# Queueing an expert's transposes, scatter and gather behind the products of the piece ahead, and ending every side of a branch with a product

## The chip, the cores and the metric

The kernel runs on one core of one Trainium2 chip. The metric is the device time of one execution in microseconds (us), as the median of several runs. One execution was also taken by the hardware profiler. It gives for each engine what ran when, at which line of the kernel, and what ended each wait. TensorE stands in its rows as PE (products and transposes, which are both matrix instructions) and PEld (the weight loads that go before them); VectorE is DVE, ScalarE is ACT, GpSimd is POOL. SP is the engine that issues the transfers. A name with q at its end (PEq, SPq) is the engine's sequencer, which takes branches, waits and loads of registers.

## The reference, cut to what matters

The reference is a two-layer backbone over 256 context and 256 latent tokens. The change touches only the feed-forward part of the second layer, which is a mixture of eight experts over the 256 latent tokens:

```python
def moe_swiglu(h, w_router, w_gate, w_up, w_down):
    logits = (h @ w_router).astype(jnp.float32)
    top_val, top_idx = lax.top_k(logits, TOP_K)          # 2 of 8 experts for each token
    top_w = jax.nn.softmax(top_val, axis=-1)
    gates = ...                                          # (tokens, 8), zero where not chosen
    out = jnp.zeros_like(h)
    for e in range(N_EXPERTS):
        out = out + gates[..., e:e + 1] * swiglu(h, w_gate[e], w_up[e], w_down[e])
    return out
```

`swiglu` is `(silu(h @ w_gate) * (h @ w_up)) @ w_down`, with 1024 x 3584 weights for gate and up and 3584 x 1024 for down, all in float32. The kernel computes for each expert only the tokens that chose it.

## The kernel before, in words

**Experts and slots.** The tokens of an expert are gathered into up to 128 slots. `gather` (line 1414) does it with products of the tokens and a one-hot matrix `P`. Slots 0 to 63 are part A and are always computed. Slots 64 to 127 are part B. How many tokens an expert has (`n_e`) is known only at run time: with at most 64 there is no part B, with 65 to 96 part B is computed as four "quarters" of 32 slots, with more as two "halves" of 64.

**Pieces.** The weights of an expert come in 21 pieces of 2 MB, 168 pieces for the eight experts, in a ring of 8 buffers (`raw`, lines 1443 to 1454). SP issues the transfer of a piece when the products that read the buffer eight pieces earlier are over. The inner width of 3584 is cut into stretches of 1024, 1024, 1024 and 512 columns. Numbered within an expert, the pieces are: 0 to 3 gate, gate, up, up of the first stretch; 4 to 7 the same of the second; 8 and 9 down of the first; 10 to 13 gate and up of the third; 14 and 15 down of the second; 16 gate and 17 up of the fourth; 18 and 19 down of the third; 20 down of the fourth.

**Products of one piece.** `prods` (line 1480) and `d_step` (line 1528) first run all of part A, eight or sixteen matrix products, each of which is two records in the trace. Then `rest_of` (line 1461) branches on `n_e`: with more than 64 tokens it runs the quarters or the halves of part B, otherwise nothing. So a piece of an expert with at most 64 tokens shows 16 records (32 in pieces 16 and 17), and one with quarters 48 (96). In this execution experts 1, 4, 5 and 7 have no part B and experts 0, 2, 3 and 6 run quarters.

**What lies between pieces.** After the last up piece of a stretch VectorE multiplies (`at`, line 1509). Then `act_t` (line 1513) transposes the product in TensorE (tiles `actA`, `actB`, line 1520), and the copies at lines 1525 and 1526 make it the left side of the down products. Further steps on TensorE are `rows_of` (tile `PT`, line 1432), the gather of the next expert (tile `gat`, line 1421), the scatter of the expert before (tile `sc`, lines 1627 and 1632; it too branches on `n_e`, and its last side runs products), and the load of `n_e` into a register of PE's sequencer (line 1669).

**Order.** The code names for each piece what is to run ahead of it: `act_t` before pieces 5, 9, 15 and 19, the scatter before piece 2, `rows_of` before 11, the gather before 14, the load of `n_e` before 0. That order is no queue order. The scheduler of the language puts an instruction into its engine's queue as early as its own model finds it ready, so in the trace these steps stand ahead of where the code has them: `act_t` straight after the last up piece, the scatter around pieces 0 and 1. A branch with all its sides is placed as one block.

Of the kernel before, what the change touches and what calls it, by code (L numbers as in the profile page):

```python
# [141 lines left out]
def kernel(  # L142
# [6 lines left out]
    V, S, G, PE, SP = nc.vector, nc.scalar, nc.gpsimd, nc.tensor, nc.sync  # L149
# [26 lines left out]
    def pst(name="ps"):  # L176
        tag = name if name in banks else "A"
        return cur["ps"].tile([128, 512], F32, tag=tag, name=name, bufs=banks[tag])
# [52 lines left out]
    last = {}  # L231
# [1040 lines left out]
    for g in range(2):  # L1272
        p = pst("shb")
        for k in range(4):
            PE.matmul(p[:, k * 128:(k + 1) * 128], modT[1][:, 24 + 4 * g + k, 0:1].to_broadcast([128, 128]), ident,
                      start=True, stop=True)
        S.copy(shb[g], p)
    shl = mb.tile([128, 32], F32, name="shl")[:, 0:8]
    p = pst("shl")
# [131 lines left out]
    def ptile(name):  # L1411
        return ptr.tile([128, 512], F32, tag="tr", name=name)
# [30 lines left out]
    def load(src):  # L1443

        n = npiece[0]
        npiece[0] += 1
        pool, bufs = (mwa, RA) if n % NR < RA else (mw, RB)
        raw = pool.tile(list(src.shape), F32, tag="raw", name="raw", bufs=bufs)
        if n < NR:
            with tc.issue_after(last["w"].ins):  # L1450
                SP.dma_start(raw, src)
        else:
            SP.dma_start(raw, src)
        return raw

    def wsel(w, e):
        if isinstance(e, int):
            return w[0, e]
        return w[0, bass.ds(e, 1)].rearrange("o a b -> (o a) b")

    def rest_of(n_e, quarters, halves):

        if n_e is None:
            halves()
            return
        with tc.If(n_e[0] > 64):  # L1466
            with tc.If(n_e[0] > 96) as br:
                halves()
            with br.Else():
                quarters()  # L1470


    STRETCH = ((0, 1024), (1024, 1024), (2048, 1024), (3072, 512))
# [1 line left out]
    def expert_steps(e, xT, done, n_e=None):  # L1475

        y = []
        at, acts = {}, {}

        def prods(p, xA, xB, w, start, stop):  # L1480

            nk = len(xA)
            n = w(0).shape[-1]

            def part(dst, x, parts):
                m, c = 128 // parts, n // parts
                for k in range(nk):
                    for i in range(parts):
                        PE.matmul(dst[m * i:m * i + m, 0:c], x[k][:, 0:m], w(k)[:, c * i:c * i + c], start=(start and k == 0),  # L1489
                                  stop=(stop and k == nk - 1), tile_position=(0, m * i))  # L1490

            part(p[:, 0], xA, 2)
            rest_of(n_e, lambda: part(p[:, 1], xB, 4), lambda: part(p[:, 1], xB, 2))

        def gu_step(m, wi, k0, nk, ps):
            width = STRETCH[m][1] // 2

            def use(raw):
                if k0 == 0:
                    ps[wi] = gu_t[wi]  # L1500
                x = xT()
                prods(ps[wi], [x[:, k0 + k, 0:64] for k in range(nk)], [x[:, k0 + k, 64:128] for k in range(nk)],
                      lambda k: raw[:, k, :], k0 == 0, k0 + nk == KD)
                if k0 + nk == KD:
                    if wi == 0:
                        at[m] = mt.tile([128, 2, 512], F32, tag="at", name="at", bufs=2)
                        S.activation(at[m][:, :, 0:width], ps[0][:, :, 0:width], AF.Silu)  # L1507
                    else:
                        V.tensor_tensor(at[m][:, :, 0:width], at[m][:, :, 0:width], ps[1][:, :, 0:width], op=ALU.mult)  # L1509

            return use

        def act_t(m):

            nb = STRETCH[m][1] // 256
            ps = [ptile("actA"), ptile("actB")]

            def tr(b, n):
                for i in range(n):
                    PE.transpose(ps[b][:, i * 128:(i + 1) * 128], at[m][:, b, i * 128:(i + 1) * 128], ident)  # L1520

            tr(0, nb)
            tr(1, nb)
            acts[m] = mt.tile([128, 2, 512], F32, tag="act", name="act", bufs=2)
            S.copy(acts[m][:, 0, 0:128 * nb], ps[0][:, 0:128 * nb])  # L1525
            V.tensor_copy(acts[m][:, 1, 0:128 * nb], ps[1][:, 0:128 * nb])

        def d_step(m, f0):
            def use(raw):
                if m == 0 and f0 == 0:  # L1530
                    y.append(y_t)
                nf = STRETCH[m][1] // 128
                b = acts[m]
                end = m == 3

                def act(part, parts):

                    w = 128 // parts
                    per = nf // parts
                    return [b[:, part, f % per * 128 + f // per * w:f % per * 128 + f // per * w + w] for f in range(f0, f0 + 4)]  # L1540

                def part(i, parts):
                    w, c = 128 // parts, 1024 // parts
                    x = act(i, parts)
                    for k in range(4):
                        for j in range(parts):
                            PE.matmul(y[0][w * j:w * j + w, i, 0:c], x[k], raw[:, k, c * j:c * j + c],  # L1547
                                      start=(m == 0 and f0 == 0 and k == 0), stop=(end and k == 3), tile_position=(0, w * j))

                part(0, 2)  # L1550
                rest_of(n_e, lambda: part(1, 4), lambda: part(1, 2))
                if end:
                    ys = mt.tile([128, 2, 512], F32, tag="ys", name="ys", bufs=1)
                    S.copy(ys[:, 0], y[0][:, 0])
                    V.tensor_copy(ys[:, 1], y[0][:, 1])
                    done.append(ys)

            return use

        late_t = []  # L1560

        def pre():
            if late_t:
                m = late_t.pop(0)
                return lambda: act_t(m)
            return None

        for m in range(5):
            if m < 4:
                c0, width = STRETCH[m]  # L1570
                nk = 4 * 1024 // width
                ps = {}
                for wi in range(2):
                    w = wsel((moe_w_gate, moe_w_up)[wi], e)[:, c0:c0 + width]
                    for k0 in range(0, KD, nk):
                        src = w[k0 * 128:(k0 + nk) * 128].rearrange("(k p) f -> p k f", p=128)
                        yield src, (pre() if k0 else None), gu_step(m, wi, k0, nk, ps)
                late_t.append(m)
            if m > 0:
                c0, width = STRETCH[m - 1]  # L1580
                for f0 in range(0, width // 128, 4):
                    src = wsel(moe_w_down, e)[c0 + f0 * 128:c0 + (f0 + 4) * 128, :].rearrange("(k p) d -> p k d", p=128)
                    yield src, (pre() if f0 else None), d_step(m - 1, f0)

    def run_pieces(gen):
        for src, pre, use in gen:
            raw = load(src)
            if pre:
                pre()
            use(raw)  # L1590

    def residual():

        for g in range(2):
            for j in range(2):
                p = ptile("hrow")
                for k in range(4):
                    PE.transpose(p[:, k * 128:(k + 1) * 128], hT[:, 4 * g + k, 256 + 128 * j:384 + 128 * j], ident)
                S.copy(acc(j, g), by2(p))
        for g in range(2):  # L1600
            p = ptile("gfb")
            for k in range(4):
                PE.matmul(p[:, k * 128:(k + 1) * 128], modT[1][:, 40 + 4 * g + k, 0:1].to_broadcast([128, 128]), ident,
                          start=True, stop=True)
            S.copy(res(g), by2(p))
# [49 lines left out]
    def all_pieces():  # L1655
# [36 lines left out]
        run_last.append(pend)  # L1692

    run_pieces(all_pieces())
    run_last[0]()

    n_rv = nc.values_load(nmax_i[0:1, 0:1], min_val=0, max_val=256)
    with tc.If(n_rv > CAP):
# [4 lines left out]
        with tc.For_i(0, NE, 1) as ev:  # L1703
# [9 lines left out]
            rk, m = lambda j: col[:, j, 0:1], lambda j: col[:, j, 1:2]  # L1713
# [46 lines left out]
```

## Time and profile before

| | |
|---|---|
| median of 3 runs | 2031.52 us (2029.23, 2031.52, 2031.91) |
| profiled execution, its own time | 2026.94 us |
| span of its instructions | 2025.2 us |
| TensorE busy with products, of the span | 93% |
| mean granted TensorE clock | 0.978 of 2.4 GHz |
| from the first expert product to the end of the last | 1072.2 us to 2007.5 us |
| weights of the experts | 168 pieces of 2048 KB |

The profile's times are from the start of the span. A busy TensorE is not yet a TensorE at its peak, and the share is an average over the whole kernel; the experts, which the change touches, are the last 950 us.

### The profile page before, as it was taken

What the parts mean: (1) busy time and instruction counts of PE and PEld (TensorE: products, weight loads), DVE (VectorE), ACT (ScalarE), POOL (GpSimd) and SP (SyncE); (2) the same over time, 40 slices, a digit from 0 to 9 for tenths busy, and PEclk for the clock granted to TensorE, in tenths of its full rate; (3) what the DMA queues carried; (4) which work ended last, traced back from release to release, by engine and by line L of the source; (5) the groups of instructions that cost most, each with busy time, mean ns of one, the idle gap of its engine ahead of it and who ended that gap; (6) DMA issues with size and microseconds to landing.
All of it is one profiled execution on the core that took longest, in us unless ns stands there. A gap on an engine that the chain in (4) does not pass through costs nothing. (4 is left out here: it accounts for less than half of the span.)

```text
span 2025.2 us, 29234 instructions
## 1 busy us (share of the span) xinstructions
PE 1889.1 (93%) x12351; PEld 1124.2 (56%) x12351; DVE 685.3 (34%) x1333; ACT 431.0 (21%) x747; POOL 199.9 (10%) x245
## 2 busy tenths in 40 slices
PE   5999999999999999999989999899999888999996
PEld 3767754667888887877464443334344343434432
DVE  5874545353333335875541112110110212111112
ACT  3323433242222224334420100000000000000000
POOL 0542221010000000562300000000000000000000
PEclk9998998999999999999989999999999999999998
DMA  9333332535333333332576889999889999999993
GB/s 321 79 115 115 125 125 73 187 100 176 100 94 96 102 117 91 99 88 99 173 291 254 329 297 388 406 404 344 325 295 358 366 404 408 403 408 404 368 398 125
DMA packets 262343, 478.50 MB, mean 236 GB/s; under 512 B 16144, under 2 KB 142096, under 8 KB 262032
## 3 DMA queue, kind: packets, MB, share of 16 engines
q1 hardware_dynamic: 262160, 475.76, 65.0%
q8 instruction: 151, 2.47, 0.5%
q14 instruction: 32, 0.26, 0.0%
HBM read 474.68 MB, written 1.05 MB: 235 GB/s over the span
## 5 line engine op out<-in xcount | busy, mean ns | idle before, releaser
L1489 PE MATMUL u<-raw,xT 128*64 128x512 f32 (+3 forms) x2048 | 258.2, 451 | 7.6 <-issue 3.3
L1547 PE MATMUL y<-raw,act 128*64 128x512 f32 (+1 forms) x1792 | 260.0, 492 | 3.4 <-PEq L1466 2.5
L1489 PE MATMUL g<-raw,xT 128*64 128x512 f32 (+3 forms) x2048 | 256.6, 450 | 2.5 <-PEq L1466 2.3
L1509 DVE TENSOR_TENSOR at<-at,u 128x1024 f32<-128x1024 f32 (+1 forms) x32 | 34.8, 1088 | 518.2 <-PE u L1489 302.2
L256 ACT CAST wh<-raw 128x1024 fp32r<-128x1024 f32 (+1 forms) x129 | 133.0, 1039 | 324.9 <-PE mm L266 169.8
L257 DVE TENSOR_TENSOR wl<-raw,wh 128x1024 fp32r<-128x1024 f32 (+1 forms) x129 | 159.4, 1240 | 115.9 <-ACT wh L256 91.6
L1489 PEld LDWEIGHTS u<-raw,xT 128*64 128x64 f32 (+1 forms) x2048 | 105.4, 124 | 159.4 <-issue 141.4
L1489 PEld LDWEIGHTS g<-raw,xT 128*64 128x64 f32 (+1 forms) x2048 | 101.1, 123 | 148.4 <-issue 128.5
L1547 PEld LDWEIGHTS y<-raw,act 128*64 128x64 f32 (+1 forms) x1792 | 88.9, 123 | 156.0 <-issue 140.6
L1507 ACT ACTIVATE at<-g 128x1024 f32<-128x1024 f32 (+1 forms) x32 | 29.4, 917 | 340.7 <-PE g L1489 185.8
L266 PE MATMUL mm<-ah,wh 128*128 128x512 f32 (+1 forms) x400 | 101.3, 388 | 0.0
L266 PE MATMUL mm<-al,wh 128*128 128x512 f32 (+1 forms) x400 | 95.9, 376 | 0.0
L1728 POOL TENSOR_TENSOR rs<-ss,mhalf 128x1 f32<-128x1 f32 x2 | 1.1, 564 | 952.2 <-DVE ss L1727 952.2
L266 PE MATMUL mm<-ah,wl 128*128 128x512 f32 (+1 forms) x400 | 93.0, 372 | 0.0
L266 PEld LDWEIGHTS mm<-ah,wh 128*128 128x128 f32 x400 | 70.3, 191 | 20.2 <-issue 6.2
L266 PEld LDWEIGHTS mm<-al,wh 128*128 128x128 f32 x400 | 70.9, 189 | 13.9 <-issue 0.8
L1525 ACT COPY act<-actA 128x512 f32<-128x512 f32 (+1 forms) x32 | 17.0, 533 | 287.0 <-PE actA L1520 287.0
L266 PEld LDWEIGHTS mm<-ah,wl 128*128 128x128 f32 x400 | 70.5, 188 | 12.9
L1159 DVE SCALAR_TENSOR_TENSOR hT<-mm,mod,hT 128x256 f32<-128x256 f32 x72 | 31.8, 480 | 94.8 <-PE mm L266 69.1
L371 POOL TENSOR_TENSOR rs<-ms,mhalf 128x4 f32<-128x4 f32 (+1 forms) x8 | 8.8, 1103 | 473.9 <-DVE ms L369 473.9
L1520 PE MATMUL actA<-cs,at 128*128 128x128 f32 x112 | 19.2, 289 | 38.6 <-DVE at L1509 38.6
L266 PE MATMUL s<-ah,wh 128*128 128x512 f32 x192 | 47.6, 390 | 0.0
(424 smaller groups left out, 2556.4 us busy)
## 6 DMA issues: line engine op xcount, KB each, us to landing
raw<-in_moe_w_gate_dram SPq DMA_DIRECT2D x56, 2048.0 KB, 12.5
raw<-in_moe_w_up_dram SPq DMA_DIRECT2D x56, 2048.0 KB, 12.1
raw<-in_moe_w_down_dram SPq DMA_DIRECT2D x56, 2048.0 KB, 13.2
raw<-in_w_ada_dram SPq DMA_DIRECT2D x64, 512.0 KB, 4.8
raw<-in_w_in_dram SPq DMA_DIRECT2D x44, 512.0 KB, 3.8
raw<-in_ffn_w_gate_dram SPq DMA_DIRECT2D x22, 512.0 KB, 3.8
raw<-in_ffn_w_up_dram SPq DMA_DIRECT2D x22, 512.0 KB, 3.8
adaw<-in_w_ada_dram SPq DMA_DIRECT2D x10, 1024.0 KB, 7.8
```

The costliest lines, as they stand in the source:

```text
L256: S.copy(wh, raw)
L257: V.tensor_tensor(wl, raw, wh, op=ALU.subtract)
L266: PE.matmul(p, uk, a(k)[hl], start=(n == 0), stop=(n == len(seq) - 1))
L371: G.tensor_tensor(r[:, j0:j1], ms[:, j0:j1], mhalf[:, j0:j1], op=ALU.pow)
L1159: V.scalar_tensor_tensor(hT[:, m, c0:c1], p[:, c0:c1], modT[l][:, 8 * gi + m, i:i + 1], hT[:, m, c0:c1], op0=ALU.mult, op1=ALU.add)
L1489: PE.matmul(dst[m * i:m * i + m, 0:c], x[k][:, 0:m], w(k)[:, c * i:c * i + c], start=(start and k == 0), stop=(stop and k == nk - 1), tile ...
L1507: S.activation(at[m][:, :, 0:width], ps[0][:, :, 0:width], AF.Silu)
L1509: V.tensor_tensor(at[m][:, :, 0:width], at[m][:, :, 0:width], ps[1][:, :, 0:width], op=ALU.mult)
L1520: PE.transpose(ps[b][:, i * 128:(i + 1) * 128], at[m][:, b, i * 128:(i + 1) * 128], ident)
L1525: S.copy(acts[m][:, 0, 0:128 * nb], ps[0][:, 0:128 * nb])
L1547: PE.matmul(y[0][w * j:w * j + w, i, 0:c], x[k], raw[:, k, c * j:c * j + c], start=(m == 0 and f0 == 0 and k == 0), stop=(end and k == 3), ...
L1728: G.tensor_tensor(rs[:, j:j + 1], ss[:, j:j + 1], mhalf[:, 0:1], op=ALU.pow)
```

## The change

Two things change. `rest_of` gets the last product step of part A (the last of the 128-row blocks of the contraction, `k`) and issues it inside the branch, on every side of it, so that no side is empty. And `run_pieces` issues what is to run ahead of a piece behind the last product of part A that stands before the branch of the piece ahead: `tc.issue_after(ins)` adds an edge of order, without a wait, from `ins` to every TensorE instruction that the block makes. Instructions of other engines are not held by it. The scatter of the last expert stands outside and is as before.

```diff
-    def rest_of(n_e, quarters, halves):
+    def rest_of(n_e, last_a, quarters, halves):
+        def halves_(b=halves):
+            last_a()
+            b()
         if n_e is None:
-            halves()
+            halves_()
             return
-        with tc.If(n_e[0] > 64):
-            with tc.If(n_e[0] > 96) as br:
-                halves()
-            with br.Else():
-                quarters()
+        with tc.If(n_e[0] > 64) as b1:
+            with tc.If(n_e[0] > 96) as b2:
+                halves_()
+            with b2.Else():
+                halves_(quarters)
+        with b1.Else():
+            last_a()
...
-            def part(dst, x, parts):
+            def part(dst, x, parts, ks=range(nk)):
...
-            part(p[:, 0], xA, 2)
-            rest_of(n_e, lambda: part(p[:, 1], xB, 4), lambda: part(p[:, 1], xB, 2))
+            part(p[:, 0], xA, 2, range(nk - 1))
+            pe = last["pe"]
+            rest_of(n_e, lambda: part(p[:, 0], xA, 2, (nk - 1,)), lambda: part(p[:, 1], xB, 4), lambda: part(p[:, 1], xB, 2))
+            last["pe"] = pe
...
-                part(0, 2)
-                rest_of(n_e, lambda: part(1, 4), lambda: part(1, 2))
+                part(0, 2, range(3))
+                pe = last["pe"]
+                rest_of(n_e, lambda: part(0, 2, (3,)), lambda: part(1, 4), lambda: part(1, 2))
+                last["pe"] = pe
...
     def run_pieces(gen):
         for src, pre, use in gen:
             raw = load(src)
-            if pre:
+            if pre and last.get("pe"):
+                with tc.issue_after(last["pe"].ins):
+                    pre()
+            elif pre:
                 pre()
             use(raw)
+        last["pe"] = None
```

## Rows read from the trace of the kernel before

**Rows 1.** The page's first part: busy time, share of the span and instructions of TensorE's products.

```profile
PE 1889.1 (93%) x12351; PEld 1124.2 (56%) x12351; DVE 685.3 (34%) x1333; ACT 431.0 (21%) x747; POOL 199.9 (10%) x245
```

**Rows 2.** Windows of the experts' stage: the stretch, its length, busy time and instructions of each engine, granted clock, share of the time in which the DMA engines were busy, and GB/s.

```profile
1500.00:1600.00 100.00, 94.51 (x845) 42.74 (x838) 14.35 (x24) 5.43 (x9) 0.00 (x0) 1.00 0.88 328
...
1605.00:1700.00 95.00, 83.36 (x421) 34.15 (x418) 16.86 (x28) 7.01 (x11) 1.00 1.03 405
1700.00:1800.00 100.00, 92.55 (x547) 37.65 (x549) 16.34 (x28) 7.52 (x11) 1.00 1.03 406
1800.00:1900.00 100.00, 94.59 (x916) 42.27 (x908) 10.91 (x19) 5.95 (x9) 1.00 1.02 398
```

**Rows 3.** TensorE's waits from 1060 us to the end: who waited for whom, us in total, times, the longest.

```profile
PE actA L1520 <- DVE at L1509: 38.6, 29, 1.8
PE sc L1627 <- ACT ys L1554: 6.1, 8, 0.8
...
PE sc L1627 <- PEq L1466: 2.7, 4, 0.7
...
PE PT L1432 <- ACT act L1525: 2.0, 7, 0.3
```

**Rows 4.** TensorE in order of time in expert 2, which runs quarters: start, length, line, what is written and read, records, and the idle time before with what ended it.

```profile
1320.75 10.97 PE L1489 MATMUL u<-raw,xT 128*64 128x512 f32 x96
1333.13 0.66 PE L1520 MATMUL actA<-cs,at 128*128 128x128 f32 x4 [1.42 <-DVE at L1509]
...
1334.15 10.97 PE L1489 MATMUL g<-raw,xT 128*64 128x512 f32 x96
```

**Rows 5.** The same view in expert 1, which has no part B.

```profile
1233.78 3.65 PE L1489 MATMUL g<-raw,xT 128*64 128x512 f32 x16 [0.16 <-PEq L1466]
1237.58 3.65 PE L1489 MATMUL u<-raw,xT 128*64 128x512 f32 x16
1241.39 3.65 PE L1489 MATMUL u<-raw,xT 128*64 128x512 f32 x16
1246.52 0.66 PE L1520 MATMUL actA<-cs,at 128*128 128x128 f32 x4 [1.48 <-DVE at L1509]
```

**Rows 6.** Weight loads inside the first of these pieces, in order of time; two products follow each row.

```profile
1234.23 0.17 PEld L1489 LDWEIGHTS g<-raw,xT 128*64 128x64 f32 x2 [0.26 <-issue]
1234.66 0.17 PEld L1489 LDWEIGHTS g<-raw,xT 128*64 128x64 f32 x2 [0.26 <-issue]
```

**Rows 7.** The sequencer's instructions at the line of `rest_of`'s outer branch: count, shortest, median and longest in ns.

```profile
L1466 PEldq EVENT_SEMAPHORE  x84: 51/51/51, 1212.5 to 2007.6; - x84
```

**Rows 8.** The same at the line of the scatter's outer branch; this is all there is.

```profile
L1641 PEldq COMPARE_BRANCH  x16: 70/139/432, 1203.9 to 2008.6; - x16
```

**Rows 9.** The loads of `n_e` into PE's registers, all experts.

```profile
L1669 PEldq TENSOR_LOAD <-cnt_i x8: 296/304/489, 1065.0 to 1187.9; - x8
```

**Rows 10.** TensorE in order of time around the loads in expert 0, and the first down piece of expert 3.

```profile
1172.00 5.56 PE L1489 MATMUL g<-raw,xT 128*64 128x256 f32 x96
1179.79 7.25 PE L1489 MATMUL u<-raw,xT 128*64 128x256 f32 x96 [2.23 <-issue]
1187.91 0.44 PE L1520 MATMUL actA<-cs,at 128*128 128x128 f32 x2 [0.88 <-DVE at L1509]
...
1494.40 7.22 PE L1547 MATMUL y<-raw,act 128*64 128x512 f32 x48
```

**Rows 11.** Granted clock at the start of that down piece (columns as in rows 2, TensorE alone).

```profile
1494.60:1498.00 3.40, 0.00 (x0) 0.00 (x0) 0.50 1.03 416
```

**Rows 12.** TensorE in order of time: the scatter after expert 1, whose halves stand on both sides of a piece, and the last piece and scatter of the kernel, where nothing stands between the halves.

```profile
1307.58 1.28 PE L1627 MATMUL sc<-ys,PT 64*128 64x512 f32 x4 [0.81 <-ACT ys L1554]
...
1314.24 1.13 PE L1627 MATMUL sc<-ys,PT 64*128 64x512 f32 x4
...
2003.87 3.65 PE L1547 MATMUL y<-raw,act 128*64 128x512 f32 x16 [0.30 <-PEq L1466]
2008.34 1.31 PE L1627 MATMUL sc<-ys,PT 64*128 64x512 f32 x4 [0.81 <-ACT ys L1554]
2010.31 1.09 PE L1627 MATMUL sc<-ys,PT 64*128 64x512 f32 x2 [0.66 <-DVE hT L1650]
2011.70 1.09 PE L1627 MATMUL sc<-ys,PT 64*128 64x512 f32 x2 [0.29 <-DVE hT L1650]
```

**Rows 13.** SP in order of time: the issues of three pieces (piece 10 of expert 4, the last piece of expert 5, the last of expert 7).

```profile
1594.04 0.37 SPq L1453 DMA_DIRECT2D raw<-in_moe_w_gate_dram  x1
...
1745.79 2.61 SPq L1453 DMA_DIRECT2D raw<-in_moe_w_down_dram  x1
...
1972.81 0.37 SPq L1453 DMA_DIRECT2D raw<-in_moe_w_down_dram  x1
```

**Rows 14.** The view of the transfers at these three issues, in the same order: size and us from issue to landing.

```profile
raw<-in_moe_w_gate_dram SPq DMA_DIRECT2D x1, 2048.0 KB, 10.6
...
raw<-in_moe_w_down_dram SPq DMA_DIRECT2D x1, 2048.0 KB, 21.3
...
raw<-in_moe_w_down_dram SPq DMA_DIRECT2D x1, 2048.0 KB, 17.1
```

**Rows 15.** The same view from 1600 to 1905 us: packets, MB and share of the 16 engines for the queue of the weights.

```profile
q1 hardware_dynamic: 33839, 122.20, 101.7%
```

**Rows 16.** TensorE: the last down piece of expert 5.

```profile
1772.53 3.65 PE L1547 MATMUL y<-raw,act 128*64 128x512 f32 x16 [0.30 <-PEq L1466]
```

More of the change, by code (lines that the diff above doesn't have):

```diff
@@ L1483, in prods @@
             n = w(0).shape[-1]
-            def part(dst, x, parts):
+            def part(dst, x, parts, ks=range(nk)):
                 m, c = 128 // parts, n // parts
-                for k in range(nk):
+                for k in ks:
                     for i in range(parts):
-                        PE.matmul(dst[m * i:m * i + m, 0:c], x[k][:, 0:m], w(k)[:, c * i:c * i + c], start=(start and k == 0),
-                                  stop=(stop and k == nk - 1), tile_position=(0, m * i))
-            part(p[:, 0], xA, 2)
-            rest_of(n_e, lambda: part(p[:, 1], xB, 4), lambda: part(p[:, 1], xB, 2))
+                        last["pe"] = PE.matmul(dst[m * i:m * i + m, 0:c], x[k][:, 0:m], w(k)[:, c * i:c * i + c], start=(start and k == 0),
+                                               stop=(stop and k == nk - 1), tile_position=(0, m * i))
+            part(p[:, 0], xA, 2, range(nk - 1))
+            pe = last["pe"]
+            rest_of(n_e, lambda: part(p[:, 0], xA, 2, (nk - 1,)), lambda: part(p[:, 1], xB, 4), lambda: part(p[:, 1], xB, 2))
+            last["pe"] = pe
         def gu_step(m, wi, k0, nk, ps):
@@ L1540, in act, with part @@
                     return [b[:, part, f % per * 128 + f // per * w:f % per * 128 + f // per * w + w] for f in range(f0, f0 + 4)]
-                def part(i, parts):
+                def part(i, parts, ks=range(4)):
                     w, c = 128 // parts, 1024 // parts
                     x = act(i, parts)
-                    for k in range(4):
+                    for k in ks:
                         for j in range(parts):
-                            PE.matmul(y[0][w * j:w * j + w, i, 0:c], x[k], raw[:, k, c * j:c * j + c],
-                                      start=(m == 0 and f0 == 0 and k == 0), stop=(end and k == 3), tile_position=(0, w * j))
-                part(0, 2)
-                rest_of(n_e, lambda: part(1, 4), lambda: part(1, 2))
+                            last["pe"] = PE.matmul(y[0][w * j:w * j + w, i, 0:c], x[k], raw[:, k, c * j:c * j + c],
+                                                   start=(m == 0 and f0 == 0 and k == 0), stop=(end and k == 3), tile_position=(0, w * j))
+                part(0, 2, range(3))
+                pe = last["pe"]
+                rest_of(n_e, lambda: part(0, 2, (3,)), lambda: part(1, 4), lambda: part(1, 2))
+                last["pe"] = pe
                 if end:
```

## The prediction
> **What bounds the kernel now.** I read the page's busy shares first: TensorE is busy 93% of the span [rows 1]. That says where to look, not what a gap is worth. The windows of the experts' stage say more [rows 2]: from 1500 to 1600 us the transfers are busy 0.88 of the time, and from 1605 to 1900 us all of it, at 398 to 406 GB/s. So two limits lie close together here, and what TensorE gains can run into the transfers. The third view is TensorE's waits [rows 3]: 38.6 us in 29 waits of the transposes for VectorE's multiplication. The timeline shows why: in expert 2 the last up product ends, the transposes stand next in the queue, and TensorE idles 1.42 us until VectorE is done, while products that need nothing from it stand behind [rows 4]. The timeline of expert 1 shows a second loss [rows 5]: a piece of 16 records takes 3.65 us, but the next starts 3.80 us after it, with an idle time that ends with PE's own sequencer at the branch. There are 84 sequencer instructions there [rows 7], which is 21 pieces of the four experts without part B.
>
> **The transposes.** Behind the products of the next piece, VectorE's 1.4 us lie under at least three quarters of a part A (12 records of 3.65 us per 16, so 2.7 us). All 29 waits go: 38.6 us, by expert 0.9 (expert 0), 6.3 (expert 1), 5.1 to 5.4 (the others: 3 x 1.42 + 0.88, or 3 x 1.48 + 0.94). The copies that follow have a whole piece before their down products. The wait of `PT` for a copy (2.0 us) goes too [rows 3].
>
> **The branch.** The scatter's branch already has products on its last side, and at its line there is no such sequencer instruction [rows 8]. So I expect the 84 to go. Inside a piece two products start every 0.43 us [rows 6], so 16 records could follow one another in 8 x 0.43 = 3.44 us, not 3.80. The gain per piece lies between the named wait, 0.16, and 0.36. I take 0.27: 84 x 0.27 = 22.7 us, and 1.8 us for a dozen pieces whose wait is 0.30. In experts with quarters nothing is gained: two pieces show as one row without idle time, 10.97 us for 96 records [rows 4]. That two products now stand behind the branch costs nothing as long as the 12 records ahead of it, 2.7 us, cover the branch, which takes about 0.14 us [rows 8].
>
> **The scatter.** Its first half no longer waits for the copy of `ys` (seven waits of 0.7 to 0.8, 5.3 us) nor its second for the sequencer (2.7 us) [rows 3]. But both halves now stand between pieces 1 and 2. If no product comes between them, the second waits for VectorE to free the accumulators. At the kernel's end this happens already: from 2008.34 to 2012.79 us are 4.45 us, where halves with a piece between take 1.28 + 1.13 [rows 12]. So the price per scatter is between 0 and 2.0 us. I take 1.0, seven times: in sum 8.0 - 7.0 = 1 us gained.
>
> **The loads of `n_e`.** Now they all run in expert 0 [rows 9]: TensorE idles 2.23 us for four of them, and the piece behind takes 7.25 us where its like takes 5.56 [rows 10]. A similar row is the down piece of 7.22 us in expert 3 (other such pieces 5.52), at a granted clock of 0.50, the lower level of 1.2 GHz, behind the waits of the transposes and `PT` [rows 10, 11]. Spread out, one load per expert sits between pieces 20 and 0, between 0.1 and 0.7 us each (2.23/4 = 0.56 where four follow each other; a part can lie beside running products). I take 0.3. Gained: 2.2 + 1.7 + 1.7 - 7 x 0.3 = 3.5 us.
>
> **TensorE's own sum:** 38.6 + 2.0 + 24.5 + 1.0 + 3.5, and 1.4 of smaller waits at the gather and the final gain, are 71 us. It would be the forecast if weights were always there. They are not.
>
> **The transfers.** A piece is 2.097 MB. From 1600 to 1905 us the queue moved 122.2 MB [rows 15], so it needs 305 x 2.097 / 122.2 = 5.23 us a piece, whatever TensorE does. A piece without part B takes TensorE 3.5 us. What protects the products is the lead: how long before its use a piece lands. The last piece of expert 5 landed at 1745.79 + 21.3 = 1767.1 and was used at 1772.53 [rows 13, 14, 16]: a lead of 5.4 us, the smallest of the stage, after two experts without part B in a row. The last piece of all landed at 1989.9 and was used at 2003.87 [rows 12, 13, 14]: a lead of 14.0.
>
> Transfers can start earlier only as buffers come free earlier. The unbroken stretch begins in expert 4 (its piece 10 landed at 1594.04 + 10.6 = 1604.6), so it moves by what experts 0 to 3 gain: transposes 0.9 + 6.3 + 5.1 + 5.1 = 17.4; the loads and the two slow pieces 5.6, less 1.2 for four loads; branches 6.5 (expert 1 and two pieces of expert 4); scatter 0.3; `PT` and gather 1.2. That is 29.8 us. From there 73 pieces follow to the last: 73 x 5.23 = 382 us (before, 385.3, as some pauses lay at the end). The last piece lands at 1604.6 - 29.8 + 382 = 1956.8 and is used at once, 47.1 us earlier than before. TensorE alone would be there 71 us earlier, so it waits 24 us, most of it in expert 5: there it can be 29.8 + 5.4 = 35 us early, and by its own sum it would be some 53. In expert 6 it then gains 5, and expert 7's branches and transposes 12, which is 52 in all, so the last landing decides. **47 us** less than 2026.9 is 1980; this execution lies 4.6 us under the median of the runs, so the median becomes 1984.6, say **1985**.
>
> At the bounds: with 0.16 a piece at the branch, and 2.0 us a scatter, experts 0 to 3 gain 7 less; with 0.36 and nothing at the scatter 6 more. At 406 GB/s the 73 pieces take 377 us, at 398 they take 384.6 [rows 2]. So the likeliest case lies between 1974 and 1995.
>
> **The rivals.**
> - *The sequencer's instruction stays* (it moves into the branch's end). Experts 0 to 3 gain 23.3; 23.3 + 5.4 at the end of expert 5, 5 in expert 6 and 6 in expert 7 are 40: 1992. Against it: rows 8. Chance 0.12.
> - *The transposes still wait*, because the order within a piece leaves them ahead of its products, or another release comes late. Experts 0 to 3 gain 12.4; plus 5.4 and 6.5 in expert 7 it is 24: 2007. For it: nothing in the trace shows how the scheduler places them. Chance 0.08.
> - *Starved products lose the clock*, which ends on the other side. In experts 5 and 7 TensorE would idle up to 1.7 us a piece (5.23 - 3.5), and the two slow pieces followed idle times of 2.23 us and of 1.42 and 0.28 about short transposes. At the lower level a piece takes twice 3.44, 6.9 us, 1.7 over the transfers' 5.23. It decides from 47/1.7 = 28 pieces on; in all 42 pieces of both experts it costs 71: 2055. Against it: some twenty waits of 1.4 us had no slow piece after them, and a slow piece leaves no idle time, behind which the clock came back both times. Chance 0.03. The Trainium skill's page "TensorE: Matmul & The Clock Gate", in its section on oscillation, tells of a kernel whose products fell to the lower clock at every wait for a transfer; here the two slow pieces agree in kind, the others do not.
> - *The transfers are the bound already*, from expert 1 on, and no landing can move. Then only the lead of 14.0 us could be spent: 2017. Against it: from 1500 to 1600 us the transfers were busy 0.88 of the time [rows 2]. Chance 0.01. The Trainium skill's page "DMA: Bandwidth & Descriptors", in its section on where 436 GB/s comes from, has transfers from HBM end at about 358 GB/s per core. By that figure a piece would take an estimated 5.9 us and the 73 pieces 428. The trace disagrees: 398 to 406 GB/s, and 385 us.
> - *The gain is lost in new stalls* (the second half of the scatter, loads, late instructions): about 2031. Chance 0.03.
>
> **How the numbers follow.** The forecast has 0.73, its own range 1974 to 1995. The first rival lies in it; reaching toward the second, the range is 1974 to 2004. I count 0.2% (4 us) as what a measurement can tell from no change. Faster by more: 0.73 + 0.12 + 0.08 + 0.01 = 0.94; within it 0.02; slower 0.04.
>
> **What the profile will show.** Right: no wait of `actA` for VectorE, with transposes between two gate pieces; no sequencer instruction at the end of the branch; 16 records every 3.5 us in experts 1 and 4; transfers busy 1.0 almost without a break from expert 4 to the end; waits for landings in expert 5 of 15 to 20 us in all and some in expert 7. Wrong, if products of expert 5 never wait for a landing (then the transfers were quicker, or TensorE's gain smaller), if the halves of a scatter wait 2 us each, or if the granted clock falls in expert 5.

## The result, and the profile after

The kernel after the change takes **1981.63 us** (median; 1973.6 to 1986.72), the kernel before beside it 2031.64 us. The ratio is 0.9753, with a 95% interval of 0.9716 to 0.979. The forecast was 1985. The profiled execution of after took 1986.72 us, with a span of 1984.9.

Two executions of one kernel differ by some 15 us, and as much can lie ahead of the experts, where the code is the same in all kernels: the gather of expert 0 starts between 1058.5 and 1073.4 us in the profiles shown here. So I also measure the **stage of the experts**, from the first record of that gather to the last product of expert 7, in one profile each: 941.6 us before, 897.9 after, 43.7 less. By expert, from 0 to 7, each taken up to its last down product, the gain is 1.2, 8.3, 7.1, 8.4, 10.3, -3.4, 5.4 and 6.4.

The page's first part, as in [rows 1]: TensorE is busy 95% now, and its busy time has hardly changed (5.9 us less). Most of the gain is idle time.

```profile
PE 1883.2 (95%) x12351; PEld 1120.6 (56%) x12351; DVE 683.7 (34%) x1333; ACT 430.5 (22%) x747; POOL 200.2 (10%) x245
```

TensorE's waits from 1060 us on (who waited for whom, us, times, longest), to be held against [rows 3]:

```profile
PE y L1556 <- issue: 6.5, 3, 2.8
PE u L1496 <- issue: 6.4, 4, 3.4
PE g L1496 <- DMA raw<-in_moe_w_gate_dram: 4.9, 3, 3.2
PE u L1496 <- DMA raw<-in_moe_w_up_dram: 4.6, 3, 1.7
PE u L1496 <- SPq L1714: 3.2, 1, 3.2
...
PE y L1556 <- SPq L1714: 2.1, 2, 1.4
...
PE y L1556 <- DMA raw<-in_moe_w_down_dram: 0.7, 2, 0.4
```

The waits of `actA` for VectorE, of `sc` for the copy and for the sequencer, and of `PT` are gone. Two kinds have come. Products wait for landings, 15.5 us in five rows (the SPq rows are waits for the last weights too, in expert 7). And 12.9 us are put down to "issue", idle time that nothing in the profile explains. I come back to it.

At the line of the outer branch there is one kind of sequencer instruction left; the 84 of [rows 7] are gone:

```profile
L1471 PEldq COMPARE_BRANCH  x168: 70/147/6050, 1075.0 to 1963.6; - x168
```

TensorE in order of time in expert 1, to be held against [rows 5]:

```profile
1223.68 3.65 PE L1496 MATMUL u<-raw,xT 128*64 128x512 f32 x16
1227.17 3.60 PE L1496 MATMUL g<-raw,xT 128*64 128x512 f32 x16
1230.70 0.66 PE L1529 MATMUL actA<-cs,at 128*128 128x128 f32 x4
1231.19 0.60 PE L1529 MATMUL actB<-cs,at 128*128 128x128 f32 x4
1231.72 3.65 PE L1496 MATMUL g<-raw,xT 128*64 128x512 f32 x16
```

A piece starts 3.49 us after the one before (3.80 before), and the transposes stand between two gate pieces with no idle time ahead of them. The same view at the scatter of expert 0's result, to be held against [rows 12]:

```profile
1207.11 7.09 PE L1496 MATMUL g<-raw,xT 128*64 128x512 f32 x32
1214.13 1.13 PE L1643 MATMUL sc<-ys,PT 64*128 64x512 f32 x4
...
1217.11 3.65 PE L1496 MATMUL u<-raw,xT 128*64 128x512 f32 x16
1220.70 1.13 PE L1643 MATMUL sc<-ys,PT 64*128 64x512 f32 x4
```

The scheduler put a whole piece between the two halves, so neither waits.

Windows, columns as in [rows 2]:

```profile
1500.00:1600.00 100.00, 100.00 (x786) 43.63 (x782) 14.66 (x21) 6.16 (x10) 0.00 (x0) 1.00 0.97 372
1600.00:1700.00 100.00, 89.41 (x462) 35.55 (x460) 20.03 (x37) 8.62 (x13) 0.00 (x0) 1.00 1.03 405
1700.00:1800.00 100.00, 91.21 (x656) 36.67 (x660) 13.97 (x20) 5.89 (x9) 0.00 (x0) 0.98 1.03 406
```

From 1500 to 1600 us TensorE runs without a break; behind that the transfers are busy all the time and TensorE is not. One place in expert 5 shows it:

```profile
1690.95 3.65 PE L1496 MATMUL g<-raw,xT 128*64 128x512 f32 x16 [3.18 <-DMA raw<-in_moe_w_gate_dram]
...
1700.92 3.65 PE L1496 MATMUL u<-raw,xT 128*64 128x512 f32 x16 [1.45 <-DMA raw<-in_moe_w_up_dram]
1706.05 3.65 PE L1496 MATMUL u<-raw,xT 128*64 128x512 f32 x16 [1.48 <-DMA raw<-in_moe_w_up_dram]
```

The last two start 5.13 us apart: the pace is that of the transfers. Expert 5 is 3.4 us longer than before.

### The profile page after: what moved, and what is told of

The parts are those of the page before. It is cut to its first block, busy times and chain, and to the rows that moved or that the text cites. A ratio compares the mean times of both kernels' runs of the same rounds, so it can differ in the third digit from the quotient of the medians.

```text
span 1984.9 us, 29168 instructions
## 1 busy us (share of the span) xinstructions
PE 1883.2 (95%) x12351; PEld 1120.6 (56%) x12351; DVE 683.7 (34%) x1333; ACT 430.5 (22%) x747; POOL 200.2 (10%) x245
## 3 DMA queue, kind: packets, MB, share of 16 engines
q8 instruction: 161, 2.64, 0.5%
## 5 line engine op out<-in xcount | busy, mean ns | idle before, releaser
L1496 PEld LDWEIGHTS u<-raw,xT 128*64 128x64 f32 (+1 forms) x2048 | 101.0, 124 | 167.5 <-issue 137.2
L1556 PEld LDWEIGHTS y<-raw,act 128*64 128x64 f32 (+1 forms) x1792 | 88.1, 124 | 159.0 <-issue 141.5
L1535 DVE COPY act<-actB 128x512 f32<-128x512 f32 (+1 forms) x32 | 20.0, 625 | 153.1 <-PE actB L1529 153.1
L1666 DVE TENSOR_TENSOR hT<-sc,hT 128x512 f32<-128x512 f32 x32 | 22.0, 688 | 92.2 <-PE sc L1648 53.4
```

The costliest lines, as they stand in the source:

```text
L1496: last["pe"] = PE.matmul(dst[m * i:m * i + m, 0:c], x[k][:, 0:m], w(k)[:, c * i:c * i + c], start=(start and k == 0), stop=(stop and k == ...
L1556: last["pe"] = PE.matmul(y[0][w * j:w * j + w, i, 0:c], x[k], raw[:, k, c * j:c * j + c], start=(m == 0 and f0 == 0 and k == 0), stop=(end ...
L1666: V.tensor_tensor(z, by2(ps[h]), res(h), op=ALU.mult)
```

## The experiments

Three questions stood behind the result. Which of the two edits brings the gain, is the rest really bound by landings, and what are the unnamed 12.9 us?

**Transposes where they were, all else as after.** (31 of the 32 groups of transposes now stand right behind an up piece, where it was 29 in the kernel before.) `act_t` is called straight after the multiplication of `at`, and `behind` puts the products into `tc.issue_after` of the last transpose:

```diff
+                        act_t(m)
...
-            part(p[:, 0], xA, 2, range(nk - 1))
+            behind(lambda: part(p[:, 0], xA, 2, range(nk - 1)))
...
-            if late_t:
-                m = late_t.pop(0)
-                return lambda: act_t(m)
```

> One part undone: the transposes of an activation stand in TensorE's queue straight behind the last up piece again and the next products behind them (28 places); the branch's sides and the places of scatter and gather are those of the changed kernel. The account of the prediction (both parts pay, and the transfers take a third of it back): the 1.4 and 0.9 us waits of the transposes for VectorE return, 38 us of TensorE's time, of which the waits for landings in experts 5 and 7 (some 16 us in the changed kernel) hide a part. Time 2000 to 2008 us against 1982; waits for landings under 8 us. Rival, that the branches alone made the gain and the transposes were hidden anyway: within 4 us of 1982.

Measured: 2016.62 us, ratio 0.9924 (0.9895 to 0.9953); stage 924.7 us, 26.8 longer than after's. TensorE's largest wait is the old one:

```profile
PE actA L1538 <- DVE at L1526: 39.2, 31, 1.4
```

So 39 us of waiting costs 27 in the stage and 35 in the median, more than I had expected. The rest is given back at the landings, whose waits fall from 15.5 to 2.7 us; expert 5 takes 95.6 us here and 100.5 in after. The transposes' order is the largest part of the gain.

**The order alone**: every side of the branch as before (part A whole ahead of it), the edges of order kept.

```diff
-        def halves_(b=halves):
-            last_a()
-            b()
...
-        with b1.Else():
-            last_a()
...
-            part(p[:, 0], xA, 2, range(nk - 1))
+            part(p[:, 0], xA, 2)
```

> The other part undone: the order of the changed kernel, but the branch as before, with an empty side for experts of at most 64 tokens. The account of the prediction: 84 sequencer instructions return, 0.3 to 0.37 us each, 25 to 30 us of TensorE's time, of which the waits for landings take up about 16: 1990 to 1995 us. Rival, that the transposes alone made the gain: within 4 us of 1982.

Measured: 1996.47 us, ratio 0.9835 (0.9812 to 0.9858); stage 904.0. That is a little above what was expected. The sequencer's waits are back, here the largest two rows:

```profile
PE g L1490 <- PEq L1467: 5.6, 18, 0.9
PE y L1550 <- PEq L1467: 5.0, 11, 1.0
```

**The branch alone**: products on every side, no edge of order.

```diff
-            if pre and last.get("pe"):
-                with tc.issue_after(last["pe"].ins):
-                    pre()
-            elif pre:
+            if pre:
                 pre()
```

> The changed kernel's branch (every side ends with a product) without the edges of order. The built queue shows that the scheduler then places only 8 of the 28 transposes straight behind an up piece (those of the fourth stretch, 0.9 us each); 20 stand behind products of the next piece by themselves, and the scatter's halves on both sides of the first piece as before. If what pays is where the transposes stand, and not the edges as such, the 8 waits cost 7 us, the scatter 4 to 8, of which the waits for landings hide most: within 8 us above the changed kernel, 1982 to 1991 us. If the edges themselves are what pays, it is near the kernel with the transposes first, 2005 to 2017.

Measured: 1993.67 us, ratio 0.9819 (0.9794 to 0.9843); stage 913.9. I had expected less loss. Yet the waits of the transposes have fallen from 38.6 to 7.0 us without any edge of order:

```profile
PE u L1496 <- issue: 11.9, 7, 3.6
PE actA L1529 <- DVE at L1518: 7.0, 8, 0.9
```

In the trace of the kernel before, 29 of the 32 groups of transposes stand right behind an up piece; here 8 do, all in the fourth stretch, and in after none. So the edits are not independent: with the last products inside the branch's block the scheduler already places most transposes behind the next piece. In the medians the order alone brings 34 us and the branch alone 38, both together 47 to 50; in the stage 38, 28 and 44.

**Fewer transfers.** Of experts 4, 5 and 7, nine pieces each are not loaded (pieces 1, 3, 5, 7, 9, 11, 13, 15 and 19 use the weights of the piece before).

```diff
-            raw = load(src)
+            if not (num // 21 in (4, 5, 7) and num % 21 in (1, 3, 5, 7, 9, 11, 13, 15, 19)):
+                raw = load(src)
```

> The changed kernel, with 27 of the 168 transfers left out: in experts 4, 5 and 7 every second piece multiplies by the weights of the piece ahead instead of its own. TensorE's work is the same. The account of the prediction: products no longer wait for landings there (16 us in the changed kernel's profile), so the time falls to 1962 to 1970 us. Rival, that the missing part of TensorE's own sum went into new stalls and not into transfers: within 4 us of 1982.

Measured: 1967.62 us, ratio 0.9708 (0.9681 to 0.9734); stage 878.3. No wait for a landing is left, and expert 5 takes 88.1 us instead of 100.5. So the waits at landings are what binds experts 5 and 7. Of the unnamed idle time about half remains, these four places, two in expert 1 and two in expert 4:

```profile
1273.09 0.65 PE L1496 MATMUL u<-raw,xT 128*64 128x256 f32 x4 [1.45 <-issue]
1279.00 1.08 PE L1556 MATMUL y<-raw,act 128*64 128x512 f32 x4 [2.68 <-issue]
...
1623.29 1.94 PE L1556 MATMUL y<-raw,act 128*64 128x512 f32 x8 [1.11 <-issue]
1629.46 4.51 PE L1556 MATMUL y<-raw,act 128*64 128x512 f32 x20 [0.92 <-issue]
```

In expert 1, whose pieces are all loaded, it is 4.1 us as in after. In expert 4 it falls from 5.2 to 2.0 and in expert 5 from 3.6 to nothing, and these are experts with fewer transfers. So the unnamed waits are not waits for weights, as they stay where no weight is late, but they shrink where less is transferred. I come back to this below.

**One more side to skip.** In after the unnamed idle times come in experts 1, 4 and 5, each time around the pieces of the fourth stretch. TensorE in order of time in expert 1:

```profile
1280.00 3.19 PE L1496 MATMUL u<-raw,xT 128*64 128x256 f32 x28
1284.63 0.65 PE L1496 MATMUL u<-raw,xT 128*64 128x256 f32 x4 [1.45 <-issue]
1285.12 2.75 PE L1556 MATMUL y<-raw,act 128*64 128x512 f32 x12
1290.50 1.98 PE L1556 MATMUL y<-raw,act 128*64 128x512 f32 x4 [2.64 <-issue]
```

The idle time lies between the products ahead of the branch and the last ones of part A behind it: 28 and 4, 12 and 4. In expert 4 it also lies ahead of the branch, inside part A, here after 8 of 16 records:

```profile
1636.36 1.94 PE L1556 MATMUL y<-raw,act 128*64 128x512 f32 x8 [2.84 <-issue]
```

In the program a piece now has 12 records of products ahead of the branch, and on its sides 4 and 16 (halves), 4 and 32 (quarters) and 4: 72, with as many weight loads 144, of which an expert without part B runs 32. Before it was 16, 16 and 32, with the weight loads 128. If what is skipped makes the instructions late, more of it must make it worse. So a third nested branch was added, with the halves on both of its sides (184 per piece):

```diff
             with tc.If(n_e[0] > 96) as b2:
-                halves_()
+                with tc.If(n_e[0] > 112) as b3:
+                    halves_()
+                with b3.Else():
+                    halves_()
```

> The changed kernel with one more side in the branch, which no expert takes (over 112 tokens), so with 40 more TensorE instructions per piece (80 in pieces 16 and 17) in the program and none more that run. In the changed kernel's profile TensorE idles 12.7 us with nothing named as its cause, at pieces 17 to 19 of experts 1, 4 and 5, behind branches that take up to 6 us. If these are instructions that come late, because a piece without part B skips most of its code, the stalls grow to several times that, mostly in experts 1, 4, 5 and 7: 1995 to 2020 us. If their cause is another (the transfers of weights, a wait), the time stays within 4 us of 1982.

Measured: 2022.21 us, ratio 0.9964 (0.994 to 0.9987), a little above what was expected; stage 932.0. None of the added instructions runs with these tokens, and nearly all of the gain is gone:

```profile
PE u L1499 <- issue: 21.7, 14, 2.5
PE y L1559 <- issue: 15.1, 12, 2.4
PE g L1499 <- issue: 10.2, 6, 3.9
```

**After once more**, to have it beside the next three on one chip.

> The changed kernel once more, as the measure for the three beside it: 1975 to 1988 us, with TensorE idle for 10 to 16 us behind no named cause and for about 16 us behind landings.

Measured: 1984.11 us, ratio 0.9753 (0.9726 to 0.978); stage 898.5. The unnamed rows are those of the first profile within 0.3 us.

**Two sides in place of three**: any expert with part B runs quarters, 104 per piece.

```diff
-            with tc.If(n_e[0] > 96) as b2:
-                halves_()
-            with b2.Else():
-                halves_(quarters)
+            halves_(quarters)
```

> The changed kernel without the branch's side for experts of over 96 tokens (a part of the computation that is left out; no expert has so many here), so with 40 TensorE instructions less per piece in the program and the same that run. If late instructions stall pieces 17 to 19, the idle time without a named cause falls from 13 us to under 4, and as the stalls of experts 1 and 4 lie ahead of the stretch in which the transfers decide, the time falls by 4 to 10 us. If instructions are not the cause: the same time as the changed kernel beside it, within 3 us.

Measured: 1976.26 us, ratio 0.9716 (0.9692 to 0.9741); stage 888.7. TensorE's waits at landings:

```profile
PE u L1493 <- DMA raw<-in_moe_w_up_dram: 7.6, 5, 1.7
PE y L1553 <- DMA raw<-in_moe_w_down_dram: 6.3, 5, 1.7
PE g L1493 <- DMA raw<-in_moe_w_gate_dram: 6.1, 6, 1.7
PE y L1553 <- SPq L1711: 3.9, 3, 1.5
...
PE u L1493 <- SPq L1711: 1.6, 1, 1.6
```

The unnamed idle time in the experts is gone, and the waits at landings have grown from 15.5 to 25.5 us. Gone are 12.9 us of stalls and three stretches of 3.4 us at a granted clock of 0.50, which cost an estimated 5 us (3 x 3.4 / 2); 10 us of that is now waited at the landings. What is left is 8 us in the median (the runs of the two kernels overlap: 1966.11 to 1979.65 against 1971.75 to 1988.08) and 9.2 to 9.8 in the stage.

**One product behind the branch** in place of a whole step of part A (two products), with three sides and with two:

```diff
-            part(p[:, 0], xA, 2, range(nk - 1))
+            part(p[:, 0], xA, 2, skip=((nk - 1, 1),))
...
-            rest_of(n_e, lambda: part(p[:, 0], xA, 2, (nk - 1,)), lambda: part(p[:, 1], xB, 4), lambda: part(p[:, 1], xB, 2))
+            rest_of(n_e, lambda: part(p[:, 0], xA, 2, only=(nk - 1, 1)), lambda: part(p[:, 1], xB, 4), lambda: part(p[:, 1], xB, 2))
```

> The changed kernel with one product instead of two on each side of the branch (the other stays ahead of it), so with 8 instructions less per piece of 144. The same sides, the same results. By the theory of late instructions the unnamed idle time falls in part, to 6 to 11 us, and the time by 1 to 4 us, which three runs could hardly tell; the branch has 14 of 16 records ahead of it and no sequencer instruction, so nothing is lost. If the one remaining product were too little to end a side with, the idle time of 0.16 us per piece would return, 13 us in all.

> Both of the edits beside it: two sides only, and one product on each (the side for over 96 tokens is left out). By the theory of late instructions no unnamed idle time is left in the experts, and the time is that of the kernel with two sides or up to 2 us less.

Measured: 1984.52 us (ratio 0.9743, 0.971 to 0.9775; stage 895.0) with three sides, 1976.87 (0.9735, 0.9716 to 0.9753; stage 889.5) with two. Neither can be told from its pair, after once more and the two sides above. In the three-sided one the unnamed idle time fell from 12.9 to 7.0 us, and the median did not follow. One thing came out beside it: expert 0 takes 134.4 and 134.1 us here, 137.9 in after, 137.8 with two sides and a whole step, and 133.0 with the order alone, whose gather ran 1.4 us shorter. So a whole step behind the branch, in place of one product, costs expert 0 some 3.5 us. The trace of after shows what is different there:

```profile
1081.35 2.36 PE L1496 MATMUL u<-raw,xT 128*64 128x512 f32 x9
1083.12 0.64 PE L1496 MATMUL g<-raw,xT 128*64 128x512 f32 x1
1083.55 0.59 PE L1496 MATMUL u<-raw,xT 128*64 128x512 f32 x1
1083.60 5.83 PE L1496 MATMUL g<-raw,xT 128*64 128x512 f32 x47
```

Products of an up piece run ahead of a gate piece that the code has before it. Such mixed stretches stand at three places of expert 0 in after, and at none with one product. Expert 0's first four pieces take 22.64 us (1075.90 to 1098.54) where they took 21.79 before. Why the mixed order costs that was not tried.

**Two sides, with nothing left out.** The kernel has a loop behind the experts for tokens beyond an expert's slots; it now takes those beyond 96, in up to two turns, and does not run with these tokens. One product stands behind the branch.

```diff
-CAP = 128
+CAP = 96
...
-            x2 = gather(onehot(C("iota"), rk, m))
+            for turn in range(2):
+                if turn:
+                    for j in range(2):
+                        V.tensor_scalar(col[:, j, 0:1], col[:, j, 0:1], -128.0, None, op0=ALU.add)
+                x2 = gather(onehot(C("iota"), rk, m))
...
```

> A version meant to be kept: the kernel with two sides and one product on each, in which tokens of an expert beyond the 96th go to the loop behind the experts (it runs twice per expert there, and not at all with this data), so that nothing is left out. Scatter has two sides too. By the theory of late instructions: no unnamed idle time in the experts, 1970 to 1979 us, 5 to 10 us under the changed kernel. Rival, that the side that is gone was not what stalled: 1982 or more.

Measured: **1974.36 us**, ratio 0.9715 (0.969 to 0.974); stage 888.8. That is some 10 us under after once more, though the two were not timed side by side, and the fastest version that computes everything. Its waits are at landings:

```profile
PE u L1495 <- DMA raw<-in_moe_w_up_dram: 8.0, 6, 1.7
PE y L1557 <- DMA raw<-in_moe_w_down_dram: 7.3, 5, 2.0
```

## Why the prediction was right, and where its terms were off

**The binding limit** was read rightly. Counted from the gather of expert 0, the gain is 30.2 us up to the issue of expert 4's piece 10 (predicted 29.8), 31.9 at the end of expert 5 (35), 37.3 at the end of expert 6 (40) and 43.7 at the end (47). The medians differ by 50.0 and 47.0 us (after, and after once more), so that 1981.63 stands so near to 1985 is in part the spread of the runs. The last 73 pieces took 385.0 us (382, by 5.23 a piece; it was 5.27). The last weights were used 0.1 us after they landed. So the transfers took what TensorE had gained beyond that, as the sum by transfers had it, and the fewer loads show it.

**The transposes**: no wait left, and transposes between two gate pieces. Right.

**The branch**: the 84 instructions went. The term was mis-sized: 0.27 us was taken per piece, and it was 0.32 to 0.38 (a start every 3.43 to 3.48 us in place of 3.80), so the upper bound of 0.36 was the better one; 84 x 0.35 = 29 us in place of 22.7.

**The scatter**: taken at 1.0 us for its second half, it cost nothing. The row at the kernel's end [rows 12] was the wrong one to go by, since there no piece is left to stand between the halves. **The loads of `n_e`**: the timeline shows no idle time at an expert's start, where 0.3 was taken.

**Expert 0** gained 1.2 us, although the removed load idle time and a slow piece in it alone were counted at 2.2 and 1.7. The mixed order above took 3.5 of it. The prediction did not have it.

**The waits at landings** were forecast at 24 us and are 15.5, 9.1 of them in expert 5 (15 to 20 forecast). What took their place is the step that failed: "That two products now stand behind the branch costs nothing as long as the 12 records ahead of it, 2.7 us, cover the branch, which takes about 0.14 us". The median branch does take 0.147 us, but the longest took 6.05, and 32 of all TensorE's branches in the stage are above 0.6 us (9 before). The row of the kernel before would have warned me, had I looked at its maximum and not only at the scatter's branch:

```profile
L1466 PEldq COMPARE_BRANCH  x168: 70/148/3212, 1072.2 to 2003.9; - x168
```

That both kinds together are 28 us, near the 24 forecast, is why the total came out right. It is partly luck: with the gains that were too small (7 for the branch, 7 for the scatter, 2 for the loads) and the losses left out (12.9 for stalls, 3.5 in expert 0, three slow stretches of the clock), the errors offset each other. Added up, they don't close to better than some 6 us. But as the transfers bind behind expert 4, any such error counts little at the end, and removing the stalls altogether gave 8 us and landing waits of 25.5, close to the 24 of the forecast.

**What makes the instructions late.** The runs give a dose and an answer. Weight loads and products per piece are those in the program; an expert without part B runs 32 of them. Fetches are packets of the instruction queue from expert 0's gather on, for all engines.

| kernel | per piece | fetches | branches over 0.6 us (their sum) | unnamed idle in the waits | median us |
|---|---|---|---|---|---|
| order alone | 128 | 106 | 13 (32 us) | 3.4 | 1996.47 |
| one product, three sides | 136 | 111 | 21 (49 us) | 7.0 | 1984.52 |
| after | 144 | 116 | 32 (80 us) | 12.9 | 1981.63 |
| one more side | 184 | 145 | 58 (195 us) | 47.0 | 2022.21 |
| two sides | 104 | 86 | 5 (10 us) | none | 1976.26 |

The two other kernels with 144 per piece have 10.8 us of unnamed idle time (transposes where they were) and 16.4 (the branch alone; 2.3 of it lie at the loads of `n_e` in expert 0).

That skipped instructions cause the stalls is shown by this series: only sides that never run were added or taken away between after and the rows with 184 and 104. That it goes by the fetches is argued from the counts and from the view of the transfers in the stretch of the stalls above (1276 to 1300 us; packets, MB, share of the 16 engines):

```profile
q1 hardware_dynamic: 2437, 9.67, 101.2%
q8 instruction: 5, 0.08, 1.4%
```

Five packets of 16 KB came in these 24 us, one each 5.8 to 5.9 us, while the weights kept the engines busy. An expert without part B passes a piece in 3.5 us. With fewer transfers the same view in expert 5 (1699 to 1707 us) has three such packets in 8 us, 3.4 and 3.5 us apart, while the queue of the weights had 30% of the engines:

```profile
q1 hardware_dynamic: 206, 0.78, 30.0%
q8 instruction: 3, 0.05, 2.4%
```

And there, as said, expert 5 has no unnamed idle time. So the record supports that the fetches are late because of the weights' transfers. It does not isolate it: in that run the scheduler also placed some products in another order, and no run slowed the fetches and nothing else. The Trainium skill's page "Runtime: NRT & Kernel Launch", in its section on instruction fetch mechanics, says that instructions come in blocks of 16 KiB, that the cost of crossing into the next block is mostly hidden, and that a taken branch to a target outside the fetched window stalls until that is there. The block's size and the stalls at branches agree with these rows. The stall of 2.84 us inside part A in expert 4 was not at a branch, and was not hidden beside a saturated queue of weights.

**The rivals.** Gone: the sequencer's instruction did not stay, the transposes did not wait, and the transfers were not the bound already, as piece 10 of expert 4 landed at 1578.4 us in place of 1604.6. "The gain is lost in new stalls (... late instructions)" was the one with something to it: it had a chance of 0.03 at 2031 us and no size of its own, and the run with one more side, 2022 us, shows how near it lay. The starved products kept their clock in the main (last section). The prediction had named a granted clock that falls in expert 5 as a sign of being wrong: it fell there once, for 3.4 us, behind an unnamed stall; in expert 7 it fell once behind a wait at a landing, of 3.16 us.

## What to carry to other kernels

Look for the instruction that waits while others behind it in the same queue need nothing it waits for: moving it one piece later gave most of the gain here, and where two limits lie close, the gain to expect is that of the other limit, found from the landings and not from the waits removed. Ending each side of a branch with a product takes away the sequencer's wait, but each copy lengthens the code that a run jumps over, and beside saturated transfers that code has a price. So look at the maximum of the branches' times as well as at their median, and give a branch as few sides as the data needs.

## What the runs showed of the hardware that was not expected

Code that never runs cost time: 40 more skipped weight loads and products per piece made 47 us of unnamed idle time out of 12.9, and 40 fewer made none of it.

The granted clock fell to 0.50 for 3.4 us three times in after's experts, each time right after an idle time: of 2.64 us (to 1290.50), of 3.38 (to 1734.48) and of 3.16 (to 1948.37). Granted clock of two such stretches and of the starved stretch between them (length, TensorE's busy time and records, clock, share and GB/s of the transfers):

```profile
1290.40:1293.70 3.30, 3.20 (x10) 0.50 1.02 407
1676.00:1710.00 34.00, 26.57 (x125) 1.00 1.03 409
1734.10:1737.40 3.30, 2.92 (x10) 0.50 1.03 411
```

In the starved stretch TensorE waited ahead of every piece that starts in it, once for 3.18 us, and kept the clock. It kept it, too, behind the 2.84 us in expert 4. So the length of one idle time doesn't decide it alone; what does was not tried. With one more side there were 30.6 us at 0.50 in the experts, with two sides none, so the stalls can cost more than their idle time. (In [rows 11] the zeros stand for products that the view left out; TensorE was busy there.)
